# A SwiGLU trunk in float32: input products of pairs of chunks by seven block products in place of eight

## The chip, the core and the metric

The kernel runs on one core of one Trainium2 chip. The metric is the device time of one execution in microseconds, given as the median of the runs. "The span" is the time between the first and last recorded instruction of one profiled execution. Engines are named as in the profile: PE (TensorE), DVE (VectorE), ACT (ScalarE), POOL (GpSimd) and SP (SyncE); SP and POOL issue the transfers here.

## What is computed

One inference step of a trunk of two layers for 544 tokens (512 of a prompt, 32 of samples). Each layer is a SwiGLU block, a mixer (retention in the first layer, RG-LRU in the second) and another SwiGLU block, each followed by a layer norm. All is float32; the model width is 1024 and the hidden width of SwiGLU 2816.

```python
def swiglu(x, w_in, w_out):
    g, u = jnp.split(x @ w_in, 2, axis=-1)
    return (jax.nn.silu(g) * u) @ w_out

def trunk(...):
    for layer in range(DEPTH):
        x = layer_norm(ALPHA * x + 0.5 * swiglu(x, ffn1_w_in[layer], ffn1_w_out[layer]), ...)
        m = retention_mixer(x, ...) if layer % N_MIXERS == 0 else rglru_mixer(x, ...)
        x = layer_norm(ALPHA * x + m, ...)
        x = layer_norm(ALPHA * x + 0.5 * swiglu(x, ffn2_w_in[layer], ffn2_w_out[layer]), ...)
```

## The kernel before

**Layout.** Activations are feature-major: the 1024 features are 8 chunks `k` of 128 partitions, and the 544 tokens lie on the free axis in two halves of 272 (`HF`). `X` holds the input of a block as a high and a low part, `Z` the residual, and `H` in the area `ARR` the hidden chunks, high and low. A product of float32 operands is three float32r products of those parts, `mm3`: high by high, high by low, low by high, all adding in one of 8 banks of PSUM.

**Weights.** They come as units of 128x1024 float32 (512 KB, 8 tiles of 128x128). `pump` lets SP load a unit into one of 4 `raw` tiles (L445); `split` lets ACT write its high part and `low` lets DVE write its low part (`raw` minus high) into one of 6 `hl` tiles, or into one of two more in `ARR` (`ext`). Units are loaded and split in the order in which `use` first names them.

**A SwiGLU block** (`ffn`). The 22 hidden chunks of 128 come in three parts (`PARTS`). In a part, each chunk and half takes one gate and one up product of 8 steps (24 matmuls of 128x272 each); ACT makes the silu of the gate (`ev_g`), DVE multiplies (`ev_u`), ACT writes the high part of the hidden chunk, DVE the low part. Then the part's output products follow, 8 chunks `m` by two halves, n steps (3n matmuls) each for a part of n chunks. `zev` adds their results into `Z`; with the first part it makes the residual, by two DVE operations on `X`'s parts. In the first part the first four chunks run all in half 0 first and then in half 1, since half 1's layer norm (`ln`) is still on its way. In the last part the last four `m` run half 0 first, then half 1, so that half 0's layer norm runs beside half 1's products.

**Order.** The order on each engine is fixed when the program is written. `Flow` walks through the list of products (`job`, `together`, `gangs`: some products go step by step together) with a model of the engines' clocks, and everything else is a generator that is resumed when its inputs are modelled to be there. Each engine then runs its own list in order and waits by semaphores.

Of the kernel before, what the change touches and what calls it, by code (L numbers as in the profile page):

```python
# [25 lines left out]
P = 128  # L26
# [9 lines left out]
PARTS = [(0, 8), (8, 15), (15, 22)]  # L36
FH = 8
RH, DK, DV = 4, 256, 512
# [7 lines left out]
N_RAW = 4  # L46
N_HL = 6
EXT0 = 8832
# [8 lines left out]
N_EXT = 2  # L57
# [4 lines left out]
def band():  # L62
    """input chunks that feed each output chunk of the block-diagonal gates"""
# [13 lines left out]
# the recurrent block after its first projections: projections (x), gates (g), output gate (p)  # L77
# [18 lines left out]
# parameter columns  # L96
# [7 lines left out]
# constant columns  # L104
# [95 lines left out]
def build(tc, D, O):  # L200
# [9 lines left out]
    X = sbt("X", 2, KC, TOK, dt=F32R)  # L210
# [6 lines left out]
    WARM = sbt("WARM", 512, dt=mybir.dt.bfloat16)  # L217
    NCV = sbt("NCV", RC, 27)
    NLR = sbt("NLR", RC, 9)
    # work areas of the phases: float32r operands and float32 data  # L220
    AR_R, AR_F = 13696, 7860
    ARR = sbt("ARR", AR_R, dt=F32R)
    ARF = sbt("ARF", AR_F)
    banks = deque((pp.tile([P, 512], F32, name=f"bank{i}"), 0.0) for i in range(8))

# [562 lines left out]
    def ffn(l, w, g, final=False, extra=None):  # L788
# [41 lines left out]
        if extra:  # L830
            do(extra)
# [923 lines left out]
```

## Time and profile before

| | |
|---|---|
| median of 3 runs | 2389.86 us (2389.68 to 2391.5) |
| span of the profiled execution | 2387.8 us |
| PE busy | 2368.8 us (99%), 18394 matmuls |
| DVE busy | 1299.4 us (54%) |
| ACT busy | 876.6 us (37%) |
| POOL busy | 19.8 us (1%) |
| transfers of SP (q1) | 232.06 MB, 31.5% of 16 engines' span |
| granted TensorE clock | nine tenths or more of full speed in all 40 slices |

Busy time is the time in which an engine has at least one instruction under way. Matmuls overlap, so the mean duration of one is longer than the distance from one to the next; the distance is read from a window: its length by the number of matmuls in it.

### The profile page before, as it was taken

Reading aid. Unit: us, or ns where it says so; the run is one execution under the profiler, and the core shown is the slowest. Engines: PE = TensorE matmul, PEld = TensorE weight load, DVE = VectorE, ACT = ScalarE, POOL = GpSimd, SP = SyncE. Lnnn points to the kernel's source line nnn. Section 1 sums busy time; section 2 is a strip of 40 time slices with the busy share of each in tenths; the row PEclk is TensorE's granted clock in tenths of the full one; section 3 lists DMA queues with packets and bytes.
Section 4 is the critical chain, followed back from the end, with each engine's and each line's share of the span. In section 5 each row is a group of like instructions: output and inputs, shape, how many; then the busy total and the mean of one; then the engine's idle time right before and its main releaser. Section 6 shows DMA issues by size and latency. Waiting matters only on the chain.

```text
span 2387.8 us, 42745 instructions
## 1 busy us (share of the span) xinstructions
PE 2368.8 (99%) x18394; PEld 2329.8 (98%) x18394; DVE 1299.4 (54%) x2390; ACT 876.6 (37%) x1477; POOL 19.8 (1%) x51
## 2 busy tenths in 40 slices
PE   9999999999999999999999999999999999999997
PEld 9999999989899999999999999999999999999997
DVE  5343337767676777643333854333587776343336
ACT  4223223343434335422223442222358845223233
POOL 0000000000000000000000000000011000000000
PEclk9999999999999999999999999999999999999999
DMA  6222322244342543322232232322213223223221
GB/s 215 88 88 87 92 89 63 68 153 136 126 162 85 177 150 122 123 86 88 88 89 89 63 106 89 89 89 85 84 53 92 90 89 124 89 89 89 80 63 39
DMA packets 68751, 236.86 MB, mean 99 GB/s; under 512 B 7456, under 2 KB 11552, under 8 KB 68560
## 3 DMA queue, kind: packets, MB, share of 16 engines
q1 hardware_dynamic: 68016, 232.06, 31.5%
q8 instruction: 144, 2.36, 0.4%
q0 software_dynamic: 544, 2.05, 0.3%
q14 instruction: 47, 0.39, 0.0%
HBM read 212.79 MB, written 21.29 MB: 98 GB/s over the span
## 4 chain that ended last, share of the span: by engine, by line
PE 97%; DVE 2%; ACT 0%; DMA 0%; issue 0%; SPq 0%; ACTq 0%; DVEq 0%
PE bank L353 95%; PE bank L357 1%; DVE ARF L324 0%; DVE Z L315 0%; PE bank L361 0%; DVE SM L333 0%; DVE raw L319 0%; DVE Z L319 0%; DMA Z<-in_x 0%; DVE SM L315 0%; ACT ARF L296 0%; ACT SM L296 0%; DVE ARF L315 0%; DVE X L319 0%; DVE SM L337 0%
## 5 line engine op out<-in xcount | busy, mean ns | idle before, releaser
L353 PE MATMUL bank<-X,hl 128*128 128x272 f32 x8640 | 1110.4, 288 | 3.6 <-DVE ARF L324 2.4
L353 PEld LDWEIGHTS bank<-X,hl 128*128 128x128 f32 x8640 | 1094.9, 188 | 8.8 <-DVE ARF L324 3.0
L315 DVE TENSOR_TENSOR hl<-raw,hl 128x1024 fp32r<-128x1024 f32 (+1 forms) x326 | 395.7, 1220 | 424.2 <-ACT hl L296 424.0
L353 PE MATMUL bank<-ARR,hl 128*128 128x272 f32 x4632 | 601.9, 289 | 0.0
L353 PEld LDWEIGHTS bank<-ARR,hl 128*128 128x128 f32 x4632 | 589.6, 188 | 3.5 <-issue 0.8
L296 ACT ACTIVATE hl<-raw 128x1024 fp32r<-128x1024 f32 (+1 forms) x326 | 341.5, 1054 | 504.5 <-PE bank L353 445.1
L296 ACT ACTIVATE ARR<-ARF 128x272 fp32r<-128x272 f32 (+9 forms) x290 | 128.4, 450 | 487.7 <-DVE ARF L319 414.4
L353 PE MATMUL bank<-X,ARR 128*128 128x272 f32 x2304 | 300.8, 288 | 0.0
L353 PEld LDWEIGHTS bank<-X,ARR 128*128 128x128 f32 x2304 | 293.6, 188 | 0.5 <-DVE ARR L315 0.2
L353 PE MATMUL bank<-ARR 128*128 128x272 f32 (+4 forms) x1556 | 244.7, 309 | 0.0
L353 PEld LDWEIGHTS bank<-ARR 128*128 128x128 f32 (+1 forms) x1556 | 216.8, 188 | 13.5
L315 DVE TENSOR_TENSOR ARR<-ARF,ARR 128x272 fp32r<-128x272 f32 (+9 forms) x290 | 133.2, 468 | 122.8 <-ACT ARR L296 122.2
L319 DVE SCALAR_TENSOR_TENSOR ARF<-bank,ARF 128x272 f32<-128x272 f32 x176 | 77.0, 437 | 196.1 <-PE bank L353 191.5
L315 DVE TENSOR_TENSOR Z<-Z,bank 128x272 f32<-128x272 f32 (+1 forms) x238 | 115.3, 491 | 100.0 <-PE bank L353 90.5
L296 ACT ACTIVATE ARF<-bank 128x272 f32<-128x272 f32 (+4 forms) x314 | 122.5, 398 | 92.2 <-PE bank L353 43.9
L315 DVE TENSOR_TENSOR ARR<-raw,ARR 128x1024 fp32r<-128x1024 f32 (+1 forms) x74 | 88.4, 1196 | 122.4 <-ACT ARR L296 122.3
L296 ACT ACTIVATE ARR<-raw 128x1024 fp32r<-128x1024 f32 (+1 forms) x74 | 76.5, 1036 | 134.5 <-PE bank L353 129.0
L353 PEld LDWEIGHTS bank<-hl,X 128*128 128x128 f32 x768 | 93.9, 188 | 4.5 <-issue 1.7
L353 PE MATMUL bank<-hl,X 128*128 128x256 f32 x768 | 95.5, 282 | 1.2 <-DVE X L319 0.8
L296 ACT ACTIVATE ARF<-Z 128x272 f32<-128x272 f32 (+1 forms) x86 | 39.2, 458 | 108.6 <-DVE Z L315 106.7
L315 DVE TENSOR_TENSOR ARF<-ARF 128x272 f32<-128x272 f32 (+1 forms) x146 | 61.3, 446 | 4.7 <-ACT ARF L296 2.5
L315 DVE TENSOR_TENSOR Z<-Z,ARF 128x272 f32<-128x272 f32 (+1 forms) x116 | 50.7, 473 | 10.9 <-ACT ARF L296 10.4
(83 smaller groups left out, 844.2 us busy)
## 6 DMA issues: line engine op xcount, KB each, us to landing
raw<-in_win SPq DMA_DIRECT2D x173, 512.0 KB, 3.5
raw<-in_wout SPq DMA_DIRECT2D x88, 512.0 KB, 3.6
raw<-in_sret SPq DMA_DIRECT2D x32, 512.0 KB, 3.7
out_rets<-raw SPq DMA_DIRECT2D x32, 512.0 KB, 3.5
raw<-in_rwin_v SPq DMA_DIRECT2D x16, 512.0 KB, 3.6
raw<-in_rwin_kq SPq DMA_DIRECT2D x16, 512.0 KB, 3.6
raw<-in_rwin_g SPq DMA_DIRECT2D x16, 512.0 KB, 3.6
raw<-in_rwout SPq DMA_DIRECT2D x16, 512.0 KB, 4.3
```

What stands on the lines that cost most here:

```text
L296: nc.scalar.activation(out=out, in_=in_, func=func, scale=scale, **kw)
L315: nc.vector.tensor_tensor(out=out, in0=a, in1=b, op=op)
L319: nc.vector.scalar_tensor_tensor(out=out, in0=a, scalar=s, in1=b, op0=op0, op1=op1)
L353: nc.tensor.matmul(out, lhsT=a, rhs=b, start=start, stop=stop)
L357: nc.tensor.matmul(out, lhsT=a, rhs=b, start=start, stop=stop)
```

## The change

Chunks 0 to 3 of a block stay as they were. The other 18 are taken as 9 pairs. For a pair, gate and up are each a product of 2x2 blocks: the weights are split in 2 chunks by two halves of the 8 features chunks (`a11`, `a12`, `a21`, `a22`), the input in two halves of the features by the two halves of the tokens. Strassen's scheme in Winograd's form makes it of seven block products, each 4 steps (12 matmuls of 128x272) for gate and for up: `s1`, `a11`, `s2`, `a12`, `s3`, `s4`, `a22`. They use three pairs of banks, (s1, s4), (a11, a12) and (s2, s3, a22), and the later ones of a bank keep adding onto what it holds after its earlier state has been read. DVE puts the results together in `GT` and `UT` (`ev`), and `finish` makes the hidden chunks of the pair from columns of both chunks and both halves at once.

The sums of weight blocks (s1 = a21 + a22, s2 = s1 + a11, s3 = a11 + a21, s4 = s2 + a12) are made in the `raw` tiles: once the tile's own content has been split, GpSimd issues a DMA that adds the next block from DRAM onto it (`add_block`). A pair takes 4 loads, 4 such DMAs and 7 splits. The sums of the input blocks are made by `sums` once for a block; the operand of a22 takes the place of `X`'s half 1, chunks 0 to 3.

Along with this, `PARTS` becomes 8, 8 and 6 chunks; there are 6 `raw` tiles; the additional `hl` tiles serve the four plain chunks and the recurrent block alone; the load of s1 is issued two places earlier; the layer norm leaves the full float32 input in `Z` (`xf`, an ACT operation for each chunk and half), from which `zev` makes the residual by one DVE operation; and the first two output products of every part go step by step together. `X` and `ARR` are one tile, `BIG`.

```diff
-PARTS = [(0, 8), (8, 15), (15, 22)]
+PARTS = [(0, 8), (8, 16), (16, 22)]
+NE = 4
-N_RAW = 4
+N_RAW = 6
+EXT = (10880, 12928, 8704, 13056)
+AHEAD = 2
...
+    def order_loads():
+        loads.extend(u for u in units if not u["prev"])
+        for i, u in enumerate(list(loads)):
+            if u["more"] is not None:
+                loads.remove(u)
+                loads.insert(max(1, i - AHEAD), u)
...
-            if not u["state"]:
+            if u["next"]:
+                v = u["next"]
+                v["raw"] = raw
+                add_block(v, v["ap"], t)
+            elif not u["state"]:
...
+    def add_block(u, ap, t):
+        nc.gpsimd.dma_start(out=u["raw"], in_=ap, accum_op=ALU.add)
+        st["dma"] = max(st["dma"], t + 1.5, fl.pe + 1.5) + 2.0
+        u["t_raw"] = st["dma"] + 1.2
+        note("dma", (), u["raw"], u["t_raw"])
...
+        if not final and g != 4:
+            for c in range(KC):
+                yield pace()
+                z = Z[:, c, sl]
+                t = act(z, z, dep=fl.ev["x", g, c, half], func=AF.Identity, bias=pcol("ln_b", 8 * li + c))
+                fl.set(("xf", g, c, half), t)
...
-            if first and not (last and m):
+            if first and not last:
+                yield ("xf", g - 1, m, half)
+                t = stt(z, z, ALPHA, b[:, :HF], ALU.mult, ALU.add, dep=t)
+                release(b, t)
...
+        def sums():
+            yield ("lnd", g, 1) if g else 0.0
+            for c in range(KC):
+                for half in range(2):
+                    yield ("xf", g, c, half)
+            o = LNB[g].o
+            T = ar(o, 3, HK * HF).rearrange("p i (c n) -> p i c n", c=HK)
+            b11, b12, b21, b22 = (Z[:, k:k + HK, h * HF:h * HF + HF] for k in (0, HK) for h in (0, 1))
+            def parts(name, src, hi, lo, t):
+                t = act(hi, src, dep=t)
+                t = tt(lo, src, f(hi), ALU.subtract, dep=t)
+                fl.set(("tf", g, name), t)
+            t = tt(T[:, 0], b11, b12, ALU.subtract)
+            t1 = tt(T[:, 1], b12, b22, ALU.subtract)
+            parts("s1", T[:, 0], TF[:, 0, 0], TF[:, 0, 1], t)
+            yield pace()
+            t = tt(T[:, 2], b11, T[:, 1], ALU.subtract)
+            parts("s2", T[:, 2], TF[:, 1, 0], TF[:, 1, 1], t)
+            yield pace()
+            parts("s3", T[:, 1], TF[:, 2, 0], TF[:, 2, 1], t1)
+            yield pace()
+            t = tt(T[:, 0], b21, T[:, 2], ALU.subtract)
+            yield ("plain", nin)
+            parts("a22", T[:, 0], X[:, 0, 0:HK, HF:TOK], X[:, 1, 0:HK, HF:TOK], t)
...
+            def ev(form, i, b, t):
+                b = b[:, :HF]
+                yield t
+                if form == "a11":
+                    t = act(R[i], b, dep=t)
+                    fl.set(("rd", nin, j, "a12", i), t)
+                elif form == "s1":
+                    yield ("rd", nin, j, "a12", i)
+                    if j > NE:
+                        yield ("hf", nin, j - 2)
+                    t = tt(B1[i], b, R[i], ALU.add, dep=t)
+                    fl.set(("rd", nin, j, "s4", i), t)
+                elif form == "s2":
+                    yield ("rd", nin, j, "a12", i)
+                    if j > NE:
+                        yield ("hf", nin, j - 2)
+                    t = tt(B0[i], b, R[i], ALU.subtract, dep=t)
+                    fl.set(("rd", nin, j, "s3", i), t)
+                elif form == "s3":
+                    yield ("rd", nin, j, "s4", i)
+                    t = tt(B1[i], b, B1[i], ALU.subtract, dep=t)
+                    fl.set(("rd", nin, j, "a22", i), t)
+                elif form == "a22":
+                    t = tt(A1[i], b, R[i], ALU.subtract, dep=t)
+                    fl.set(("c21", nin, j, i), t)
+                elif form == "s4":
+                    yield ("rd", nin, j, "s3", i)
+                    t = tt(B0[i], b, B0[i], ALU.subtract, dep=t)
+                    fl.set(("c12", nin, j, i), t)
+                else:
+                    if j > NE:
+                        yield ("hf", nin, j - 2)
+                    if i:
+                        yield ("c11", nin, j)
+                        t = stt(A0[1], b, 0.5, A0[0], ALU.mult, ALU.mult, dep=t)
+                        fl.set(("h11", nin, j), t)
+                    else:
+                        t = act(A0[0], b, dep=t, func=AF.Silu)
+                        fl.set(("c11", nin, j), t)
+                return t
...
+            def finish():
+                for i in range(2):
+                    for k in ("c12", "c21"):
+                        yield (k, nin, j, i)
+                    yield ("rd", nin, j, "a22", i)
+                    if i == 0:
+                        ts = act(GT[:, HF:], GT[:, HF:], dep=fl.ev["c21", nin, j, 0], func=AF.Silu)
+                yield ("h11", nin, j)
+                t = stt(UT[:, HF:], UT[:, HF:], 0.5, GT[:, HF:], ALU.mult, ALU.mult, dep=ts)
+                hh, hl = H[:, 0, c:c + 2], H[:, 1, c:c + 2]
+                u2 = UT.rearrange("p (c n) -> p c n", c=2)
+                t = act(hh, u2, dep=t)
+                t = tt(hl, u2, f(hh), ALU.subtract, dep=t)
+                for m in (j, j + 1):
+                    for half in range(2):
+                        fl.set(("h", nin, m, half), t)
+                fl.set(("hf", nin, j), t)
...
+            def run():
+                fl.spawn(finish())
+                banks_of = {}
+                for form, bk in (("s1", 0), ("a11", 1), ("s2", 2), ("a12", 1), ("s3", 2), ("s4", 0), ("a22", 2)):
+                    u, mv = units_of[form], moving(form)
+                    for i in range(2):
+                        start = (bk, i) not in banks_of
+                        if start:
+                            banks_of[bk, i] = acq_main()
+                        else:
+                            fl.need(("rd", nin, j, form, i))
+                        b = banks_of[bk, i]
+                        for k in range(HK):
+                            need_unit(u)
+                            xh, xl, e = mv(k)
+                            fl.need(e)
+                            off = (HK * i + k) * P
+                            wt = u["hl"]
+                            mm3(b[:, :HF], wt[:, 0, off:off + P], wt[:, 1, off:off + P], xh, xl, start and k == 0, k == HK - 1, not start)
+                            used(u)
+                            fl.poll()
+                        fl.spawn(done(form, i, b, fl.pe + 0.1))
...
+                reg("s1", ap=win[blk["a21"]], more=win[blk["a22"]])
+                if last:
+                    last()
+                reg("a11", ap=win[blk["a11"]])
+                reg("s2", ap=win[blk["a11"]], prev=us["s1"])
+                reg("a12", ap=win[blk["a12"]])
+                reg("s3", ap=win[blk["a21"]], prev=us["a11"])
+                reg("s4", ap=win[blk["a12"]], prev=us["s2"])
+                last = lambda reg=reg, blk=blk: reg("a22", ap=win[blk["a22"]])
...
+            if hf == 0:
+                for half in range(2):
+                    gangs([x for j in js[:NE] for x in gu(j, half)], FGA if g else 1)
+                do(lambda: (fl.set(("plain", nin), fl.pe), st.update(ext=())))
+                js = js[NE:]
+            for j, us in pair_units(js[::2]):
+                pair(j, us, hf)
...
+                jobs.append(lambda m=m, half=half, hf=hf, n=n, rhs=rhs:
+                            job(wtiles(nout + str(hf), wout[hf], m * n, range(n)), rhs, half,
+                                zev(m, half, hf == 0, hf == 2, (li, g + 1, final), count, guard)))
+            gangs(jobs, 2)
```

PE, first block, chunks 4 and 5 (a row is a product: the bank it fills, its operands, the shape, and the number of matmuls). Before:

```order
L353 MATMUL bank0_81<-X_61,hl0_67 128x272 x24
L353 MATMUL bank1_82<-X_61,ARR_79 128x272 x24
L353 MATMUL bank2_83<-X_61,hl0_67 128x272 x24
L353 MATMUL bank3_84<-X_61,ARR_79 128x272 x24
L353 MATMUL bank4_85<-X_61,ARR_79 128x272 x24
L353 MATMUL bank5_86<-X_61,hl1_68 128x272 x24
L353 MATMUL bank6_87<-X_61,ARR_79 128x272 x24
L353 MATMUL bank7_88<-X_61,hl1_68 128x272 x24
```

and after, from s1 to the first of s4:

```order
L359 MATMUL bank0_81<-BIG_61,hl0_69 128x272 x12
L359 MATMUL bank1_82<-BIG_61,hl0_69 128x272 x12
L359 MATMUL bank2_83<-BIG_61,hl1_70 128x272 x12
L359 MATMUL bank3_84<-BIG_61,hl1_70 128x272 x12
L359 MATMUL bank4_85<-BIG_61,hl2_71 128x272 x12
L359 MATMUL bank5_86<-BIG_61,hl2_71 128x272 x12
L359 MATMUL bank2_83<-BIG_61,hl3_72 128x272 x12
L359 MATMUL bank3_84<-BIG_61,hl3_72 128x272 x12
L359 MATMUL bank4_85<-BIG_61,hl4_73 128x272 x12
L359 MATMUL bank5_86<-BIG_61,hl4_73 128x272 x12
L359 MATMUL bank0_81<-BIG_61,hl5_74 128x272 x12
```

Eight products of 24 matmuls became fourteen of 12 (the second of s4 and two of a22 follow), and a unit of weights now serves 24 matmuls instead of 48.

DVE, end of the first block's last input products. Before, from the last chunk's evictions (its ARR is the low part of `H`) to the first output product:

```order
L319 SCALAR_TENSOR_TENSOR ARF_80<-bank5_86,ARF_80 128x272
L315 TENSOR_TENSOR ARR_79<-ARF_80,ARR_79 128x272
L315 TENSOR_TENSOR ARR_79<-raw1_64,ARR_79 128x1024
L319 SCALAR_TENSOR_TENSOR ARF_80<-bank7_88,ARF_80 128x272
L315 TENSOR_TENSOR ARR_79<-ARF_80,ARR_79 128x272
L315 TENSOR_TENSOR Z_62<-Z_62,bank0_81 128x272
```

and after, from the last pair's evictions (GT and UT lie in ARF, `H` in BIG):

```order
L320 TENSOR_TENSOR ARF_80<-bank6_87,ARF_80 128x272
L320 TENSOR_TENSOR hl5_74<-raw3_66,hl5_74 128x1024
L320 TENSOR_TENSOR ARF_80<-bank7_88,ARF_80 128x272
L324 SCALAR_TENSOR_TENSOR ARF_80<-ARF_80 128x816
L320 TENSOR_TENSOR BIG_61<-ARF_80,BIG_61 128x1088
L320 TENSOR_TENSOR Z_62<-Z_62,bank0_81 128x272
```

The last pair's hidden chunks are now finished in one operation of 816 and one of 1088 columns behind the last eviction, where each half of a chunk was finished by itself.

## Rows read from the trace of the kernel before

**Rows 1.** The page: span, busy time (share, instructions), chain that ended last by engine

```profile
span 2387.8 us, 42745 instructions
...
PE 2368.8 (99%) x18394; PEld 2329.8 (98%) x18394; DVE 1299.4 (54%) x2390; ACT 876.6 (37%) x1477; POOL 19.8 (1%) x51
...
PE 97%; DVE 2%; ACT 0%; DMA 0%; issue 0%; SPq 0%; ACTq 0%; DVEq 0%
```

**Rows 2.** Waits of PE: engine and line waited for: us, times, longest

```profile
PE bank L353 <- DVE ARF L324: 2.4, 3, 0.9
...
PE bank L353 <- ACT X L296: 1.1, 2, 0.7
```

**Rows 3.** Windows: length, busy PE, PEld, DVE, ACT, POOL (instructions), clock, DMA, GB/s

```profile
200.00:300.00 100.00, 100.00 (x799) 100.00 (x798) 34.61 (x53) 24.37 (x35) 0.00 (x0) 1.00 0.30 90
2000.00:2300.00 300.00, 300.00 (x2392) 300.00 (x2391) 115.12 (x176) 84.03 (x127) 0.00 (x0) 1.00 0.31 94
2355.00:2374.00 19.00, 18.79 (x147) 18.41 (x145) 15.13 (x37) 8.90 (x19) 0.00 (x0) 1.00 0.13 46
```

**Rows 4.** Groups by line and shape: busy us, mean ns of one | idle before

```profile
L353 PE MATMUL bank<-X,hl 128*128 128x272 f32 x8640 | 1110.4, 288 | 3.6 <-DVE ARF L324 2.4 <-ACT X L296 0.7 <-DVE X L315 0.4
...
L315 DVE TENSOR_TENSOR hl<-raw,hl 128x1024 fp32r<-128x1024 f32 x324 | 394.3, 1223 | 420.8 <-ACT hl L296 420.6
L296 ACT ACTIVATE hl<-raw 128x1024 fp32r<-128x1024 f32 x324 | 340.3, 1057 | 502.9 <-PE bank L353 445.1 <-issue 39.8 <-DMA raw<-in_sret 8.5
...
L296 ACT ACTIVATE ARF<-bank 128x272 f32<-128x272 f32 x262 | 100.9, 389 | 84.0 <-PE bank L357 39.5 <-PE bank L353 39.4 <-DVE ARR L315 2.0
...
L315 DVE TENSOR_TENSOR ARF<-bank,ARF 128x272 f32<-128x272 f32 x76 | 29.4, 434 | 14.6 <-PE bank L357 7.4 <-PE bank L353 7.0
...
L296 ACT ACTIVATE Z<-Z,PR 128x272 f32<-128x272 f32 x15 | 8.6, 608 | 8.5 <-DVE Z L315 8.5
...
L315 DVE TENSOR_TENSOR Z<-Z 128x1088 f32<-128x1088 f32 x5 | 6.5, 1292 | 0.2
...
L296 ACT ACTIVATE Z<-Z 128x1088 f32<-128x1088 f32 x5 | 5.6, 1113 | 0.1
```

**Rows 5.** Timeline of PE behind the first block and ahead of the recurrent one

```profile
422.00 4.14 PE L353 MATMUL bank<-X,hl 128*128 128x272 f32 x30
426.53 0.50 PE L353 MATMUL bank<-hl,X 128*128 128x256 f32 x2 [0.39 <-ACT X L296]
427.84 4.42 PE L353 MATMUL bank<-hl,X 128*128 128x256 f32 x35 [0.82 <-DVE X L319]
...
1771.15 1.12 PEld L353 LDWEIGHTS bank<-X,hl 128*128 128x128 f32 x8 [0.30 <-DVE X L319]
```

**Rows 6.** Timeline of the third SwiGLU block's start (start us, us, engine, line, ...)

```profile
1349.46 2.79 PE L353 MATMUL bank<-X,hl 128*128 128x272 f32 x21
...
1373.15 1.32 DVE L319 SCALAR_TENSOR_TENSOR X<-Z,PR,X 128x272 fp32r<-128x272 f32 x3
```

**Rows 7.** DMA: queue shares (whole, then 200 to 300 us), issues, POOL's loads

```profile
q1 hardware_dynamic: 68016, 232.06, 31.5%
...
q1 hardware_dynamic: 2448, 8.91, 29.7%
...
raw<-in_win SPq DMA_DIRECT2D x14, 512.0 KB, 3.5
raw<-in_wout SPq DMA_DIRECT2D x3, 512.0 KB, 3.6
...
ARF<-in_dt POOLq DMA_DIRECT2D x4, 320.0 KB, 3.3
...
ARF<-in_cs POOLq DMA_DIRECT2D x1, 544.0 KB, 4.0
...
L1047 POOL DMA_DIRECT2D ARF<-in_dt x4: 536/537/543, 423.8 to 817.4; - x4
...
DMA to landing us min/median/max: 3.2/3.3/5.6
```

More of the change, by code (lines that the diff above doesn't have):

```diff
@@ L350, in pe, with mm @@
         h.append((0, 512, "pe", fl.pe, True))
-    def mm(out, a, b, start, stop):
-        nc.tensor.matmul(out, lhsT=a, rhs=b, start=start, stop=stop)
+    def mm(out, a, b, start, stop, cont=False):
+        nc.tensor.matmul(out, lhsT=a, rhs=b, start=start, stop=stop, skip_group_check=cont)
         pe(out, a, b, size(b), a.shape[0])
@@ L419, in split @@
         raw = u["raw"]
-        parts = [slice(i * UW // u["cut"], (i + 1) * UW // u["cut"]) for i in range(u["cut"])]
+        cut = u.setdefault("cut", 1)
+        parts = [slice(i * UW // cut, (i + 1) * UW // cut) for i in range(cut)]
         t = max(u["t_raw"], t_hl + 0.1)
@@ L698, in ev @@
                 yield ("zd", g, m, half)
-            if first and not (last and m):
+            if first and not last:
+                yield ("xf", g - 1, m, half)
+                t = stt(z, z, ALPHA, b[:, :HF], ALU.mult, ALU.add, dep=t)
+                release(b, t)
+            elif first and not m:
                 t = stt(z, f(X[:, 0, m, sl]), ALPHA, b[:, :HF], ALU.mult, ALU.add, dep=t)
@@ new lines, in pair_units, with reg @@
+        def pair_units(js):
+            res = []
+            last = None
+            for j in js:
+                n0 = 2 * NE + 2 * (j - NE)
+                blk = {"a11": n0, "a12": n0 + 1, "a21": n0 + 2, "a22": n0 + 3}
+                us = {}
+                def reg(form, key=j, us=us, **kw):
+                    us[form] = use((nin, "pair", key, form), n=2 * HK, **kw)
+                reg("s1", ap=win[blk["a21"]], more=win[blk["a22"]])
[7 more added lines that the diff above has]
+                last = lambda reg=reg, blk=blk: reg("a22", ap=win[blk["a22"]])
+                res.append((j, us))
+            last()
+            return res
@@ L830, in ffn @@
         if extra:
             do(extra)
+        do(lambda: st.update(ext=(2, 3)))
+        do(lambda: fl.spawn(sums()))
         for hf, (j0, j1) in enumerate(PARTS):
             js = list(range(j0, j1))
-            ne = 4 if hf == 0 else 0
-            order = [(j, 0) for j in js[:ne]] + [(j, 1) for j in js[:ne]] + [(j, h) for j in js[ne:] for h in (0, 1)]
             def gu(j, half):
-                return [lambda: job(wtiles(nin, win, (2 * j) * KC, range(KC), True), xrhs(g), half, ev_g(j, half)),
-                        lambda: job(wtiles(nin, win, (2 * j + 1) * KC, range(KC), True), xrhs(g), half, ev_u(hf, j, half))]
@@ L839, in ffn @@
-            for part, n in ((order[:ne], FGA if g else 1), (order[ne:], FGB if ne and g else 1)):
-                gangs([x for jh in part for x in gu(*jh)], n)
+                return [lambda: job(wtiles(nin, win, (2 * j) * KC, range(KC), (2, 3)), xrhs(g), half, ev_g(j, half)),
+                        lambda: job(wtiles(nin, win, (2 * j + 1) * KC, range(KC), (2, 3)), xrhs(g), half, ev_u(hf, j, half))]
+            if hf == 0:
[3 more added lines that the diff above has]
+                js = js[NE:]
@@ L1584, in rhs @@
                 return XH[:, 0, k, hs(half)], XH[:, 1, k, hs(half)], ("yr", k, half)
-            job(wtiles("co", D["cwout"], m * RC, range(RC), True), rhs, half, zev(m, half, True, True, (4, g + 1, False), count))
+            job(wtiles("co", D["cwout"], m * RC, range(RC), (0, 1)), rhs, half, zev(m, half, True, True, (4, g + 1, False), count))
+        do(lambda: st.update(ext=()))
     ffn(0, 0, 0)
```

117 lines of the change are left out of this document (70 added, 47 removed).

## Prediction, made before the result was known

> **What bounds the kernel now.** I read the busy shares first, then the chain of waits, then TensorE's waits. TensorE is busy for 2368.8 of the 2387.8 us, VectorE for 54%, ScalarE for 37% [rows 1], and 97% of the chain that ended last is TensorE's own [rows 1]. The time that TensorE spends waiting for another engine inside the program comes to a few us; its two largest entries that the change touches are 2.4 us and 1.1 us [rows 2]. So a removed matmul is worth one matmul pitch, as long as nothing that the change adds becomes later than TensorE. In a plain stretch of input and output products 2392 matmuls take 300.00 us and in another 799 take 100.00 [rows 3]: 125.4 and 125.2 ns each, at a granted clock of 1.00 (the level of 2.4 GHz). The mean duration of 288 ns in the grouped row [rows 4] is not the price, since matmuls overlap. In such a stretch VectorE works 38%, ScalarE 28% and the DMA engines 31% of the time [rows 3], so there is room, though not without end.
>
> The span is 2387.8 us, and the median of the runs 2389.9: about 2.1 us lie outside the span. I make the sum against the span and add 2.1.
>
> **1. Matmuls removed.** A pair of chunks took 2 chunks x 2 products x 2 halves x 24 = 192 matmuls of 128x272 and takes 7 x 24 = 168. There are 9 pairs in each of four SwiGLU blocks: 36 x 24 = 864 fewer. 864 x 125.4 ns = **-108.3 us**. Everything removed was on the path, so this is also the most that the change can give: 2389.9 - 108.3 = 2281.6.
> The row puts the pitch of 272 columns at 125.4 ns. The Trainium skill, "TensorE: Matmul & The Clock Gate", section "Back-to-back issue gap", gives N/2.4 + 2.5 ns for a single warm matmul, 115.8 ns here; by it this term would be an estimated -100.1 us. The trace disagrees by 8% and decides.
>
> **2. The end of each part.** Output products need the hidden chunks. Before, the last chunk's gate and up were evicted product by product; now a pair's four chunks of results become final only after the last product (a22), and then come in a row a VectorE eviction (434 ns), a product of 816 columns (between the 434 ns of 272 and the 1292 ns of 1088: 1.0 us), ScalarE's high part of 1088 (1.11 us) and VectorE's low part of 1088 (1.29 us) [rows 4]: 3.8 us, and about 4.2 with the weight split of 1.22 us that the order puts between the evictions. Cover: the two first output products go step by step together, so (n-2) chunks x 2 x 3 matmuls stand ahead of the first one that needs the pair. For parts of 8 chunks that is 36 x 0.1254 = 4.5 us, which hides it; for the part of 6, 24 x 0.1254 = 3.0, short by 1.2. Four blocks: **+4.8** (0 if the split isn't in the way and ScalarE answers at once, 30 if every one of the 12 part ends loses 2.5).
>
> **3. A shorter last part (7 chunks to 6).** The layer norm of half 0 is covered by the last four products of half 1. They shrink by 4 x 3 = 12 matmuls, 1.5 us. TensorE already waits there: 0.39 and 0.82 us behind the first block, 0.30 us ahead of the recurrent block [rows 5]; so what is taken from the cover is waited for. There are three such places, of which I charge two in full: **+3.0** (0 to 4.5). At the kernel's end the seven last products shrink by 21 matmuls, 2.6 us, while VectorE is busy for 15.13 of 19.00 us there [rows 3]; half of it: **+1.3** (0 to 2.6).
>
> **4. The residual.** Z gets the layer norm's bias on ScalarE (64 more operations of 608 ns [rows 4], 38.9 us) and 80 VectorE operations leave. The first 32 of them stand between the layer norms of the two halves. There is little slack: half 1's last chunks of X are written until 1374.5, and half 0's four plain chunks, started at 1349.46 [rows 6], last 192 x 0.1254 = 24.1 us, until 1373.5. I take 0.75 us at each of four norms: **+3.0** (0 to 10).
>
> **5. Sums of activations.** The operands of s1, s2, s3 and a22 are sums of quarters of the input, made after half 1's norm and needed after 4 plain chunks in both halves (48.2 us: from 1349.5 to 1397.7). From 1374.5 that leaves 23 us; the eight bias operations of half 1 (4.9 us) and four rounds of 1.29 + 1.11 + 1.29 us make about 20 when nothing else runs between. Tight, **+1.0** (0 to 6).
>
> **6. Splits and evictions of a pair.** 108 more weight splits (7 instead of 4 for each pair). One pair lasts 168 x 0.1254 = 21.07 us. VectorE in it: 7 x 1.223 + 11 evictions x 0.434 + 1.0 + 1.29 = 15.6 us; ScalarE: 7 x 1.057 + 2 copies x 0.389 + about 1.2 for two silus + 1.11 = 10.5. Neither is full. A bank is written again after three groups of 12 matmuls, 4.5 us behind the end of the group that must be evicted first; an eviction takes 0.43 and may stand behind two splits (2.4). Taken at **0**; if it isn't covered, one split of 1.22 us for each pair shows up (rival C).
>
> **7. The accumulating DMAs.** 144 of them, 4 for each pair, issued by GpSimd; no row of before shows one. From below: a plain load of 512 KB by SyncE lands after 3.5 us, GpSimd's plain loads of 320 and 544 KB after 3.3 (3.2 to 5.6) and 4.0, with 0.54 us of issue [rows 7]. The share of a plain load in the 16 engines is 0.297 x 100 us / 17 loads = 1.75 us [rows 7]. From above I have nothing but the work itself: the destination must be read as well as written, and the pieces may go slower. The weights of a pair pass through the chain: s1 split (1.06 + 1.22), accumulate (L), s2 split, accumulate (L), s4's high part, then the next pair's s1. This is 2 x (2.3 + L) + 1.1, and stays below 21.07 while L, from readiness to landing, is up to **7.7 us**. In engine time: 4 x 1.75 + 4a, below 21.07 while a is up to **3.5 us**, twice a plain load. I take L = 4 to 6 and a = 1.75 to 3.5, nearest to GpSimd's own rows: hidden, **0**. If a pair takes more, the products made ahead help: six split buffers hold up to 5 of a pair's 7 splits at a part's start, 10 to 15 us. A gain isn't to be had here: TensorE is not waiting for weights now.
>
> **Sum.** -108.3 + 4.8 + 3.0 + 1.3 + 3.0 + 1.0 = -95.2: span 2292.6, time **2295**.
>
> **Rivals.**
> (A) The accumulate costs exactly twice a plain load. Then the DMA engines have 7.0 + 14.0 = 21.0 us of work in a pair's 21.07, against 31% now, and a load or an accumulate stands behind another one: one plain load (1.75 us) uncovered in every third pair is 36 x 0.58 = 21 us: **2316**. For it: the destination is a second operand. Against: the lead at part starts. By the Trainium skill, "Collectives: The Full Stack", section "The bandwidth ceiling: the fold count and why AG ≠ RS ≠ AR", an add in a DMA needs two source reads for each chunk and runs at half the rate of a copy; no row here shows it.
> (B) Slower: the accumulate costs three times a plain load (5.25 us) or lands after some 11 us. A pair takes 28.0 us, 6.9 more than its matmuls. Part by part (2, 4 and 3 pairs) with 10 us of lead each: 3.8 + 17.6 + 10.7 = 32.1, in four blocks 128 us: 2295 + 128 = **2423**. It decides where 9 pairs lose 23.8 + 30 us in a block: 6.0 for each pair, a pair of 27.0, that is a = 5.0 us or L = 10.7. TensorE would wait for splits whose ScalarE half waits for a DMA. For it: no row of the operation. Against: plain loads land in 3.5 to 4.0.
> (C) A jam in the queues: in the fixed order VectorE and ScalarE stand at a split whose sum hasn't landed, and the evictions behind it come late; one split of 1.2 us for each pair: 36 x 1.2 = 43, **2338**.
> (D) The change does not do what it says: shorter groups (12 matmuls for 24) cost TensorE at each change of bank. 36 x 14 = 504 groups would have to lose 0.19 us each to eat the gain: **2390**. Against: in the stretch of 2392 matmuls the changes of bank are in the pitch, and runs of 30 show no idle time between them [rows 3, 5].
>
> **How the numbers follow.** Forecast 0.66, A 0.13, C 0.08, B 0.11, D 0.02. The range goes from the full gain without a stall (2281) to C (2338): B, D and a little beyond either end are left out, together under 0.2. About 0.2% (5 us) is what a measurement of this kernel can tell from no change. Faster: forecast, A and C, with a part of D: 0.88; the same 0.01; slower: B, 0.11.
>
> **What would show it.** 864 fewer matmuls of 128x272 at 125 ns (1). A wait of TensorE, about 1.2 us, for VectorE's low part at the first output product of each third part, and none at the others (2). Longer waits for X behind the norms (3, 4) and at the first s1 or a22 of a block (5). Pairs in 21.1 us, with VectorE 74% busy (6). Accumulates that land within 7.7 us, with ScalarE's splits not waiting for them on the path, and a queue of GpSimd whose engine time is 144 x 1.75 to 3.5 us (7). Wrong would be: a pair much longer than 21.1 us (B, C), or a pitch in pairs above 125 ns (D).

## The result and the profile after

The changed kernel takes 2353.1 us (2351.3 to 2355.2 in four runs) against 2390.5 us: a ratio of 0.984, with a 95% interval of 0.983 to 0.986. It is 37 us faster, where 95 were forecast; 2353.1 lies above the stated range of 2281 to 2338. The page of the profiled execution:

```profile
span 2351.3 us, 41831 instructions
...
PE 2289.0 (97%) x17530; PEld 2238.5 (95%) x17530; DVE 1532.3 (65%) x2630; ACT 1021.0 (43%) x1557; POOL 143.5 (6%) x195
...
q1 hardware_dynamic: 68016, 232.06, 30.0%
q0 software_dynamic: 21280, 77.56, 19.4%
...
PE 89%; DVE 7%; ACT 3%; issue 1%; DMA 0%; SPq 0%; ACTq 0%; DVEq 0%
...
raw<-in_win POOLq DMA_DIRECT2D x144, 512.0 KB, 5.7
```

The 864 matmuls are gone (18394 to 17530), and against [rows 1] TensorE's share of the chain fell from 97% to 89%: 10% of it is VectorE and ScalarE now, and none is DMA. TensorE's waits say who:

```profile
PE bank L359 <- ACT BIG L301: 20.8, 17, 6.7
PE bank L359 <- DVE BIG L320: 12.3, 14, 0.9
PE bank L359 <- ACT ARF L301: 5.7, 4, 3.2
```

BIG holds the operands of matmuls. In [rows 2] the largest such wait was 2.4 us in three pieces; now the first two are 33 us in 31 pieces, in front of operands that ScalarE (high parts) and VectorE (low parts) finish late. The next view is of windows (length, busy time of PE, PEld, DVE, ACT and POOL with instructions, granted clock, DMA share, GB/s), first a stretch of nothing but pairs, then five in which TensorE waits:

```profile
160.00:230.00 70.00, 70.00 (x559) 70.00 (x558) 47.44 (x66) 33.16 (x40) 8.70 (x10) 1.00 0.74 184
100.00:110.00 10.00, 8.71 (x68) 8.28 (x67) 5.37 (x7) 4.00 (x4) 0.87 (x1) 1.00 0.77 192
350.00:360.00 10.00, 7.19 (x39) 6.60 (x39) 4.90 (x8) 2.08 (x5) 0.56 (x1) 0.83 0.38 129
410.00:420.00 10.00, 7.29 (x36) 6.89 (x35) 9.99 (x25) 4.48 (x9) 0.00 (x0) 0.66 0.13 34
1370.00:1380.00 10.00, 5.53 (x45) 5.31 (x43) 5.10 (x8) 6.16 (x11) 1.41 (x2) 0.94 0.69 112
1380.00:1390.00 10.00, 7.08 (x33) 6.77 (x34) 8.75 (x10) 5.77 (x7) 0.00 (x0) 0.55 0.37 118
```

Within the pairs nothing waits: 559 matmuls in 70.00 us are 125.2 ns each, as in [rows 3], with VectorE at 68%, ScalarE at 47% and the DMA engines at 74%. All the loss lies in a few places between them, and the granted clock, which was 1.00 before up to the last matmuls, falls behind the longer waits.

To find those places, take the time from the start of each matmul to the start of the next, less the pitch of its shape in undisturbed stretches, and add it up. Over the run this sum is 71 us larger after than before; 864 pitches are 108.3, and the tail behind the last matmul grew by 1.4: 108.3 - 71 - 1.4 = 36, the difference of the two spans (2387.8 - 2351.3 = 36.5). The 71 us by place, what the low clock takes from the matmuls included:

| place | lost more than before | of it clock | forecast |
|---|---|---|---|
| ends of the 12 parts (8 x 1.8, 4 x 3.3 to 4.9) | 32.3 | 3.2 | 4.8 |
| start of the third block, 1375 to 1403 | 15.5 | 3.8 | 1.0 for all four blocks |
| starts of the second and fourth blocks | 4.3 | | in the 1.0 |
| layer norms (410, 895 to 931, 1325, 1723 to 1748) | 14.6 | 2.6 | 3.0 + 3.0 |
| start and end of the kernel, and what is too small to place | 4.5 | 1.5 | 1.3 |

### The profile page after: what moved, and what is told of

It is laid out like the page before. It is cut to its first block, busy times and chain, and to the rows that moved or that the text cites. A ratio compares the mean times of both kernels' runs of the same rounds, so it can differ in the third digit from the quotient of the medians.

```text
span 2351.3 us, 41831 instructions
## 1 busy us (share of the span) xinstructions
PE 2289.0 (97%) x17530; PEld 2238.5 (95%) x17530; DVE 1532.3 (65%) x2630; ACT 1021.0 (43%) x1557; POOL 143.5 (6%) x195
## 3 DMA queue, kind: packets, MB, share of 16 engines
q0 software_dynamic: 21280, 77.56, 19.4%
## 4 chain that ended last, share of the span: by engine, by line
PE 89%; DVE 7%; ACT 3%; issue 1%; DMA 0%; SPq 0%; ACTq 0%; DVEq 0%
PE bank L359 87%; DVE hl L320 1%; PE bank L363 1%; ACT hl L301 1%; ACT BIG L301 1%; DVE ARF L320 1%; DVE BIG L320 1%; DVE ARF L324 1%; DVE Z L324 1%; DVE Z L320 1%; ACT ARF L301 0%; DVE ARF L329 0%; DVE BIG L324 0%; DVE SM L338 0%; PE bank L367 0%
## 5 line engine op out<-in xcount | busy, mean ns | idle before, releaser
L359 PE MATMUL bank<-BIG,hl 128*128 128x272 f32 x15096 | 1949.7, 290 | 44.0 <-ACT BIG L301 18.9
L359 PEld LDWEIGHTS bank<-BIG,hl 128*128 128x128 f32 x15096 | 1920.5, 189 | 63.9 <-ACT BIG L301 22.7
L320 DVE TENSOR_TENSOR hl<-raw,hl 128x1024 fp32r<-128x1024 f32 (+1 forms) x490 | 596.1, 1221 | 493.6 <-ACT hl L301 491.0
L301 ACT ACTIVATE hl<-raw 128x1024 fp32r<-128x1024 f32 (+1 forms) x490 | 514.1, 1055 | 751.3 <-PE bank L359 572.1
L320 DVE TENSOR_TENSOR BIG<-ARF,BIG 128x272 fp32r<-128x272 f32 (+11 forms) x198 | 136.6, 702 | 103.2 <-ACT BIG L301 102.6
L320 DVE TENSOR_TENSOR ARF<-bank,ARF 128x272 f32<-128x272 f32 (+3 forms) x460 | 186.0, 436 | 14.6 <-PE bank L363 7.9
L359 PE MATMUL bank<-BIG 128*128 128x272 f32 (+5 forms) x1172 | 194.1, 316 | 0.2 <-DVE ARF L329 0.2
L359 PEld LDWEIGHTS bank<-BIG 128*128 128x128 f32 (+3 forms) x1172 | 167.9, 188 | 13.8 <-DVE ARF L329 0.7
L359 PE MATMUL bank<-hl,BIG 128*128 128x256 f32 (+2 forms) x1024 | 146.6, 300 | 2.7 <-ACT BIG L301 1.9
L359 PEld LDWEIGHTS bank<-hl,BIG 128*128 128x128 f32 (+1 forms) x1024 | 127.3, 179 | 13.9 <-ACT BIG L301 2.1
L301 ACT ACTIVATE ARF<-Z 128x272 f32<-128x272 f32 (+1 forms) x86 | 39.4, 458 | 103.8 <-DVE Z L320 101.1
```

The source lines that it names most:

```text
L301: nc.scalar.activation(out=out, in_=in_, func=func, scale=scale, **kw)
L320: nc.vector.tensor_tensor(out=out, in0=a, in1=b, op=op)
L359: nc.tensor.matmul(out, lhsT=a, rhs=b, start=start, stop=stop, skip_group_check=cont)
```

## The experiments

The theory was that these are separate short chains of VectorE and ScalarE that TensorE waits for, each to be mended by itself. The rival was that the stream of weights (DMA, splits) is late as a whole, and that a wait that is taken away comes back at the next place. Times are medians; the changed kernel has 2353.1. (The expectations, written before this table, count half of each stretch at the low clock as lost. TensorE was idle in part of them, so that 18.5 us at the third block there are 15.5 here.)

### The end of a part

The timeline of VectorE, then ScalarE, then TensorE, at the end of the first part (start us, length us, engine, line, operation, count, idle time before and what ended it):

```profile
99.33 0.78 DVE L320 TENSOR_TENSOR ARF<-bank,ARF 128x272 f32<-128x272 f32 x2
101.15 1.23 DVE L320 TENSOR_TENSOR hl<-raw,hl 128x1024 fp32r<-128x1024 f32 x1 [1.03 <-ACT hl L301]
102.29 0.43 DVE L320 TENSOR_TENSOR ARF<-bank,ARF 128x272 f32<-128x272 f32 x1
102.83 1.01 DVE L324 SCALAR_TENSOR_TENSOR ARF<-ARF 128x816 f32<-128x816 f32 x1
105.01 1.29 DVE L320 TENSOR_TENSOR BIG<-ARF,BIG 128x1088 fp32r<-128x1088 f32 x1 [1.18 <-ACT BIG L301]
```

```profile
100.05 1.06 ACT L301 ACTIVATE hl<-raw 128x1024 fp32r<-128x1024 f32 x1 [1.90 <-PE bank L359]
101.02 0.87 ACT L301 ACTIVATE ARF<-ARF 128x816 f32<-128x816 f32 x1
103.87 1.11 ACT L301 ACTIVATE BIG<-ARF 128x1088 fp32r<-128x1088 f32 x1 [1.98 <-DVE ARF L324]
```

```profile
93.72 10.96 PE L359 MATMUL bank<-BIG,hl 128*128 128x272 f32 x86
105.03 0.39 PE L359 MATMUL bank<-BIG,hl 128*128 128x272 f32 x1 [0.36 <-ACT BIG L301]
106.36 0.89 PE L359 MATMUL bank<-BIG,hl 128*128 128x272 f32 x5 [0.94 <-DVE BIG L320]
```

The pair's last product is done at about 100.2. VectorE stands at a weight split whose high part ScalarE makes only then (100.05 to 101.1), and the eviction that everything waits for comes behind it, at 102.29. The chain is over at 106.3: 6.1 us, not 4.2. Two ways to mend it, one on either side.

**More cover (e1).**

```diff
-            gangs(jobs, 2)
+            gangs(jobs, 4)
```

> The first four output products of each part go step by step together, in place of the first two. Theory: the lost time at the ends of parts is a chain of 6.2 us behind the last product of a pair (eviction, product, high part, low part, with a weight split in between), of which the cover hides 4.5 us (8 chunks) or 3.0 us (6 chunks). Four products make the cover 9.0 and 6.0 us: the eight waits of 1.72 us go, the four of 3.24 us shrink to 0.2, and the clock doesn't fall behind them (3 x 1.7 us): 13.8 + 12.2 + 5.1 = 31 us less than the changed kernel, 2322. Rival: TensorE there follows a stream of weights or evictions that is late as a whole; then the wait moves behind the gang and the time stays within 5 us of 2353.

Measured: 2332.2 us, 21 less. The eight waits of 1.72 us are gone, and of the four of 3.24 no more than 0.3 is left, as the theory said. But in the last part TensorE now waits longer for the layer norm of half 0, here for the first of three:

```profile
380.83 0.62 PE L363 MATMUL bank<-ARF,CT 128*128 128x272 f32 x2
385.60 0.51 PE L359 MATMUL bank<-hl,BIG 128*128 128x256 f32 x2 [4.16 <-ACT BIG L301]
```

At the first norm this only takes the place of the 7 us that the changed kernel loses there (at 410); at the second and third norm 6.1 and 3.1 us more are lost than in the changed kernel, the low clock included, and another 4.6 in the mixer behind the first block (476 to 492). The start of the third block, which wasn't edited, loses 5.9 less. Together these make most of the 10 us by which the gain falls short. The rival, that the wait moves behind the gang, doesn't hold for the part ends; it holds for the last part, in another form.

**A shorter chain (e2).** `hold` is set at the start of a part's last a22 and cleared behind the pair's low part; `pump` begins no split while it is set.

```diff
+            if st["hold"]:
+                break
```

> No weight split is begun between the start of a part's last a22 product and the end of the pair's low part. Theory: the split between the two evictions of a22 costs the chain about 2 us, since VectorE stands at it until ScalarE has made its high part; without it the chain is 4.2 us, the eight ends of 8 chunks lose 0 in place of 1.72, the four of 6 chunks 1.3 in place of 3.24, and the clock falls less: 20 to 26 us less than the changed kernel, 2327 to 2333, unless the delayed split of output weights is itself missed. Rival: the four steps of the chain alone are longer than they were taken, then no more than 5 us.

Measured: 2329.3 us, 24 less, inside the range. VectorE and ScalarE at the same place now:

```profile
97.92 1.29 DVE L320 TENSOR_TENSOR ARF<-bank,ARF 128x272 f32<-128x272 f32 x3
98.80 0.89 ACT L301 ACTIVATE ARF<-ARF 128x816 f32<-128x816 f32 x1 [2.05 <-DVE ARF L320]
99.72 1.01 DVE L324 SCALAR_TENSOR_TENSOR ARF<-ARF 128x816 f32<-128x816 f32 x1 [0.51 <-ACT ARF L301]
100.76 1.11 ACT L301 ACTIVATE BIG<-ARF 128x1088 fp32r<-128x1088 f32 x1 [1.08 <-DVE ARF L324]
...
101.91 1.29 DVE L320 TENSOR_TENSOR BIG<-ARF,BIG 128x1088 fp32r<-128x1088 f32 x1 [1.18 <-ACT BIG L301]
```

The chain runs through without a split. At the eight ends of 8 chunks the loss is 0.0 to 0.2 us, at the four of 6 chunks 1.5, where 1.3 was worked out: some 25 us less at the ends in all. New losses of 1.4 to 1.8 us at 481, 1006 and 1152 take a part of it back. The mis-sized term was the split.

**Three together in the last part alone (e9, on top of e8 below).**

```diff
-            gangs(jobs[:8], 2)
+            gangs(jobs[:8], 3 if hf == 2 else 2)
```

> The three edits of e8 and, in the last part alone, three output products step by step together in place of two. Theory: without a split in it the chain of a pair is 4.2 to 4.5 us, and three products of the part of 6 chunks cover 4.5 us: the four waits of 1.5 us that e8 still has there go, 6 us less than e8, 2318, with the norms' waits as they are. Rival: more products together shift work out of the cover of the second norm, as four did (4.3 us at three norms in place of 2), then the same or up to 6 us more than e8.

Measured: 2331.3, 7 us more than e8, a little beyond the rival's 6. The rival was right in kind: the 6-chunk ends lose next to nothing any more, and TensorE waits 4.2 us for the norm at 381 and 3.4 at the two others, with 6.8 us at the low clock behind each. The norm that is late is half 0's, as in e1. The traces show where its time goes. VectorE in e9, at the eviction of half 0's last output product (Z) and the steps behind it, then the same eviction in the changed kernel:

```profile
373.04 1.22 DVE L320 TENSOR_TENSOR hl<-raw,hl 128x1024 fp32r<-128x1024 f32 x1 [2.18 <-ACT hl L301]
374.18 0.43 DVE L320 TENSOR_TENSOR Z<-Z,bank 128x272 f32<-128x272 f32 x1
...
376.12 2.36 DVE L320 TENSOR_TENSOR hl<-raw,hl 128x1024 fp32r<-128x1024 f32 x2 [0.68 <-ACT hl L301]
```

```profile
381.33 0.44 DVE L320 TENSOR_TENSOR Z<-Z,bank 128x272 f32<-128x272 f32 x1 [1.00 <-PE bank L359]
```

In the changed kernel the eviction follows its product at once, and one weight split stands among the norm's steps; in e9 the eviction stands behind a split that waits for ScalarE, and more splits stand behind it. That is what the ends of parts showed, at another place. No run kept the splits away from there, so what they cost at the norms is read from the traces and not shown by an experiment.

### The start of the third block

The lines of VectorE, ScalarE and TensorE in the changed kernel, in order of time:

```profile
1377.08 0.51 ACT L301 ACTIVATE Z<-Z,PR 128x272 f32<-128x272 f32 x1
...
1379.71 2.48 DVE L320 TENSOR_TENSOR ARF<-Z 128x1088 f32<-128x1088 f32 x2
1381.03 1.11 ACT L301 ACTIVATE BIG<-ARF 128x1088 fp32r<-128x1088 f32 x1 [2.49 <-DVE ARF L320]
...
1382.19 0.60 PE L359 MATMUL bank<-BIG,hl 128*128 128x272 f32 x1 [6.66 <-ACT BIG L301]
...
1394.65 1.28 DVE L320 TENSOR_TENSOR ARF<-Z,ARF 128x1088 f32<-128x1088 f32 x1
1395.97 1.11 ACT L301 ACTIVATE BIG<-ARF 128x1088 fp32r<-128x1088 f32 x1 [6.58 <-DVE ARF L320]
...
1398.36 5.81 PE L359 MATMUL bank<-BIG,hl 128*128 128x272 f32 x32 [3.24 <-ACT ARF L301]
```

The last bias operation on Z ends at 1377.6; fourteen of the sixteen run after half 1's norm, from 1353.1 on, in between evictions and splits. The first sum follows at 1379.7, and TensorE, which needs its high part, has waited 6.7 us. Between 1389.4 and 1394.6 VectorE works through some 28 small operations (10 columns, 0.17 us each), the rates of the recurrent block, which the kernel before also computes here; behind them comes the fourth sum, ScalarE stands 6.6 us at that sum's high part, and the eviction of a11 is behind ScalarE's stand.

**The rates elsewhere (e4).** `lru_rates` among the first part's output products:

```diff
+            if extra and hf == 0:
+                do(extra)
```

> The small computation of the recurrent block's rates (28 VectorE operations on 10 columns, two table loads) leaves the start of the third block and stands among the output products of its first part. Theory: at 1388 to 1394.5 it stands in front of the fourth sum on VectorE, whose high part holds up ScalarE's copy of a11 behind it; without it the wait of 3.4 us and one stretch at the low clock (1.7 us) go: 5 us less than the changed kernel. The first wait of 6.8 us stays. Rival: the fourth sum waits for the end of the plain products anyway, then 0.

Measured: 2350.6, 2.5 less, which is no more than the spread of the runs; the trace tells more. The second wait went (the block's start lost 10.5 us in place of 15.5), the first stayed at 6.8; but the moved operations cost 3.5 us where they went, in front of the next part's first pairs (0.98, 1.29 and 0.95 us between 1528 and 1553).

**The bias operations at once, at all norms (e3).**

```diff
-                yield pace()
```

> The sixteen operations that put the bias onto Z are issued right behind each half's layer norm, without spacing. Theory: the sums of input blocks in the third block come 7 us late because the bias operations before them are spread over 24 us behind evictions and splits; issued at once the sums are early enough, and the waits of 6.8 and 3.4 us at 1375 and 1395 with the low clock behind them (18.5 us in all) go, those of 1 to 2 us in the second and fourth block too; the norms may lose up to 4 us as ScalarE is occupied between the halves: 12 to 20 us less than the changed kernel. Rival: the work of the sums itself is what is too long, then within 4 us of it.

Measured: 2367.0, 14 us more: the forecast had the wrong sign. The wait at 1375 did go, so the late bias operations were its cause. But new waits came: 6.8 us at 1397, where the rates now stand on VectorE in front of the first pair's evictions, 2.2 and 3.1 at the start of the fourth block, 2.1 at the second's. The first of them:

```profile
1404.34 1.96 PE L359 MATMUL bank<-BIG,hl 128*128 128x272 f32 x7 [6.61 <-DVE ARF L320]
```

With the low clock behind them they are more than what was won.

**The bias operations at once, at the third block alone (e10), with e2's `hold`; and the same with the rates moved (e8).**

```diff
+                if g != 3:
+                    yield pace()
```

> As e8, but the rates are computed where the change leaves them, at the start of the third block. Theory: the two waits in the third block have two causes, the late bias operations (about 9 us with the low clock) and the rates on VectorE and their table loads on ScalarE (5 us or more): 2329 - 9 = 2320 to 2326, near e8, since the moved rates cost e8 3.6 us among the output products. Rival: both waits have one cause, then the same as e2 (2329) or more.

> Three edits together: no split behind a part's last a22 (2329 by itself), the rates computed among the first output products of the third block, and the bias operations of the norm ahead of the third block at once. Theory: the three waits are separate ones. The third block's start, which lost 18.5 us, keeps 3 to 5; the moved rates cost 3 where they go: 2329 - 14 + 3 = 2318, or 2315 to 2322. Rival: with the bias operations at once the splits and evictions of the first pair come late instead (as with all four norms at once), then 2327 or more.

Measured: e10 2324.9 and e8 2323.9, a ratio of 0.9725 (0.971 to 0.974) to the kernel before: 66 us less than before and 29 less than the changed kernel, the least of those run. e10 is inside its range, e8 missed its own (2315 to 2322). Both are 4 to 5 us below e2 (2329.3) with runs that overlap, so what they add to `hold` rests on the traces more than on the times. Of the changed kernel's 15.5 us at this place, e10 keeps 11.7, most of it in one wait with the low clock behind it. Its VectorE and its TensorE:

```profile
1377.80 0.17 DVE L329 TENSOR_SCALAR SM<-SM 128x10 f32<-128x10 f32 x1 [0.33 <-ACT SM L301]
...
1382.87 0.25 DVE L329 TENSOR_SCALAR SM<-SM 128x10 f32<-128x10 f32 x2
1383.03 1.13 DVE L320 TENSOR_TENSOR ARF<-bank,ARF 128x272 f32<-128x272 f32 x3
```

```profile
1383.87 2.41 PE L359 MATMUL bank<-BIG,hl 128*128 128x272 f32 x9 [7.78 <-DVE ARF L320]
```

The evictions of the first pair stand behind the rates, and TensorE behind the evictions. e8 has two waits of 2.1 and 2.8 us in its place, 9.3 us lost with the clock; it pays 3.6 us where the rates are now and 3.2 in a new wait at the second block's start. So the two causes are separate, as e4 and e3 said, but what they give doesn't add up. That the planner orders the queues anew with each edit is the likely reason; it was not shown.

### The layer norms

**The last part of 6 without the rest (e5).** The kernel before, with

```diff
-PARTS = [(0, 8), (8, 15), (15, 22)]
+PARTS = [(0, 8), (8, 16), (16, 22)]
```

> The kernel before with parts of 8, 8 and 6 chunks in place of 8, 7 and 7, nothing else. Theory: a last part of 6 takes 1.5 us from the cover of the layer norm of half 0 at three places, where TensorE waits already, and 2.6 us from the cover of the last norm: 3 to 6 us more than before (2393 to 2396), and a stretch at the low clock behind a longer wait would add 1.7 to 3.4. Rival: the norms' cover has slack that the waits of before don't show, then within 1 us of before.

Measured: 2395.1, a ratio of 1.002 (1.001 to 1.003) to before, 5.2 us more. TensorE at the norm behind the first block in this kernel:

```profile
428.04 0.50 PE L353 MATMUL bank<-hl,X 128*128 128x256 f32 x2 [1.90 <-ACT X L296]
429.35 2.87 PE L353 MATMUL bank<-hl,X 128*128 128x256 f32 x13 [0.81 <-DVE X L319]
```

against 0.39 and 0.82 in [rows 5], and a stretch of 3.4 us at the low clock behind it. The changed kernel has the same two waits at the same place, to the digit:

```profile
412.10 0.50 PE L359 MATMUL bank<-hl,BIG 128*128 128x256 f32 x2 [1.90 <-ACT BIG L301]
413.41 10.84 PE L359 MATMUL bank<-hl,BIG 128*128 128x256 f32 x66 [0.81 <-DVE BIG L324]
```

The shorter part is the whole cause of the waits there. What the clock adds differs: 3.4 us at the lower level behind them in e5, 6.8 in the changed kernel.

**The bias operations between the norms (e11).** As e2, with half 0's bias operations behind half 1's norm:

```diff
+            if not half:
+                yield ("lnd", g, 1)
```

> As e2, but the eight bias operations of half 0 wait until half 1's layer norm is done, so that ScalarE has none of them between the two norms. Theory: they cost the second half's norm little (under 1 us at each of four norms), since ScalarE waits for VectorE there, while the sums become later still: e2 plus 0 to 6 us. Rival: they are what holds the second half's norm (2.06 and 2.17 us at 402 and 924), then 4 to 8 us less than e2.

Measured: 2336.8, 7 us more than e2, 1 beyond the range. The waits at the norms are the same (1.90 and 0.81 at 404 to 407, 2.17 at 925); the first of them in this run:

```profile
405.90 0.50 PE L359 MATMUL bank<-hl,BIG 128*128 128x256 f32 x2 [1.90 <-ACT BIG L301]
```

So the bias operations do not hold the norms. They hold the sums: the start of the second block now loses 7.6 us in place of e2's 3.7.

### The accumulating DMAs

**Plain loads in their place (e6); each twice (e7).** The sums of weights aren't made in e6, and are other sums in e7, so neither computes the trunk.

```diff
-        nc.gpsimd.dma_start(out=u["raw"], in_=ap, accum_op=ALU.add)
+        nc.gpsimd.dma_start(out=u["raw"], in_=ap)
```

> GpSimd's 144 accumulating transfers are plain loads of the same blocks into the same tiles, so the sums of weights aren't made; all else is the changed kernel. Theory: the accumulates are hidden in the pairs (5.7 us to landing, below 7.7; 3.1 us of the engines each), so their price is next to nothing: 0 to 5 us less than the changed kernel, the small part at the first pairs of a block where ScalarE waits for them. Rival: the traffic of the accumulates is what makes operands late at the ends of parts and at the blocks' starts, then 20 us or more less.

> Each accumulating transfer is issued twice in a row onto the same tile, so the sums of weights are other ones. Theory: a pair hides accumulates until they land after 7.7 us or fill the engines. Twice in a row they land after 11 us, a pair's chain of splits takes 2 x (2.3 + 11.4) + 1.1 = 28.5 us and the engines 4 x 1.6 + 8 x 3.1 = 31 us, against 21.07 of matmuls; with 10 us of lead in each part 150 to 250 us more than the changed kernel, with TensorE waiting for splits. Rival: the lead of loads and splits is larger than 10 us for each part, then under 60 us more.

Measured: e6 2352.1, 1.0 less than the changed kernel, which is within the spread of the runs; its TensorE waits are the same. Queue of GpSimd and landing in e6:

```profile
q0 software_dynamic: 21280, 77.56, 10.5%
...
raw<-in_win POOLq DMA_DIRECT2D x144, 512.0 KB, 3.9
```

With 77.56 MB being 148 units of 512 KB (144 of them these transfers), a plain load takes 0.105 x 2348.5 / 148 = 1.67 us of the engines and an accumulate 0.194 x 2351.3 / 148 = 3.08, that is 1.85 times; it lands 1.8 us later (5.7 against 3.9) and TensorE doesn't see it.

e7 took 2880.4 in its one run, 527 us more, twice what the theory gave. TensorE waits for what ScalarE and VectorE make, and ScalarE for transfers:

```profile
PE bank L359 <- ACT ARF L301: 263.7, 37, 13.0
PE bank L359 <- DVE ARF L320: 126.8, 25, 6.5
...
ACT hl L301 <- DMA raw<-in_win: 891.3, 105, 15.3
```

The mechanism is the one expected, and the formula of the chain holds: two accumulates in a row (6.4 us to landing each, 0.9 of issue) make L about 13.7 and a pair 33 us, 12 more than its matmuls, which is 430 us for 36 pairs. The rest is the low clock (0.91 mean granted), which takes some 110 us more from the matmuls than in the changed kernel. What was wrong was the lead of 10 us for each part: the first block's second part, with four pairs, ends 197 us behind the first part's end, against 135 in the changed kernel, 15.5 more for each pair with the clock, so there is next to none.

## Why the prediction was wrong

The direction and the largest term were right, the size was not. Of the 58 us between 2295 and 2353.1, term 2 made 27.5, term 5 made 18.8, the norms (terms 3 and 4) 8.6, and the start, the end and what is too small to place 3.2; 11 us of all this are the clock's. Each of the two large misses by itself would have left the time within the range, whose upper end was rival C's alone and not a sum of the terms' upper bounds.

**1, the matmuls**: right. 864 fewer, at 125.2 ns in the pairs. The formula of the Trainium skill ("TensorE: Matmul & The Clock Gate", "Back-to-back issue gap"), an estimated 115.8 ns, is for a single matmul; the pairs, a stream, don't show it either. Rival D is answered too: with 12 matmuls to a group the pitch is the same.

**2, the ends of parts**: the step that failed most, 32.3 for 4.8. The four operations of the chain were sized rightly (0.43, 1.01, 1.11, 1.29 us). "About 4.2 with the weight split that the order puts between the evictions" was wrong: the split was charged about 0.4 us, and it costs 2, because VectorE doesn't only execute it but stands at it until ScalarE has made its high part, which itself starts only when TensorE gives an `hl` tile free. The order of instructions showed the split between the two evictions; what it didn't show is whose finish it waits for. The row of that operation in [rows 4] did: before 324 of them VectorE stood idle for 420.8 us, 420.6 of it for ScalarE, 1.3 us each. With 6.1 us in place of 4.2, all twelve ends lose, where four were charged. The term passed the upper bound of 30 that the prediction gave it, with the 3.2 us of the clock in it.

**3, the shorter last part**: 3.0 + 1.3 forecast; by itself, in the kernel before, 5.2. Right in mechanism and near in size, though not for the reasons given alone: at the norm behind the first block e5 loses 3.0 us more than before, 1.5 by the waits, as worked out, and the other 1.5 by the clock. In the changed kernel the norms lose 14.6; what of it is beyond this term (some 4 us at 895 to 931, behind the retention, and more at 1723 to 1748 than e5 has there) was not taken apart.

**4, the residual**: the place was wrong. The bias operations cost the norms nothing (e11); they cost the block's start, since the sums wait for all sixteen of them, and fourteen, where term 5 counts eight, ran behind half 1's norm.

**5, the sums**: 19.8 for 1.0, beyond the bound of 6. Two things failed. The 23 us of cover were compared with the work of the chain (20 us when nothing else runs), and the words "when nothing else runs between" were the error: evictions, splits and the sixteen bias operations share the two queues, and at the third block the recurrent block's rates too, which stand in the code of before at the same place and were not looked for.

**6, splits and evictions inside a pair**: right, 0. Rival C was about the wrong place: such jams exist, but at the first pair of a block and the last pair of a part, where queues are full of other work, not in each pair.

**7, the accumulating DMAs**: right, 1 us or nothing. L is 5.7 and a 3.08. Rival A's premise (twice a plain load) nearly holds at 1.85 times, and yet it costs nothing, since the engines are at 0.74 of their time in a pair. The half rate that the Trainium skill ("Collectives: The Full Stack", "The bandwidth ceiling: the fold count and why AG ≠ RS ≠ AR") gives for an add in a collective is near the 1.85 times of this case. Rival B's decision point was too lenient: it counted on a lead that e7 doesn't show.

**The clock** was in no term, without a reason given. At the kernel's start and at waits of 2 to 7 us in one piece, or several close together, it was granted at the lower level (1.2 GHz) for 3.4 to 10.2 us, 34 us in all up to the last matmul; the matmuls in them took 11 us longer than at full speed. That added 1.1 us to each of three part ends that waited 3.2 us, 3.8 to the 11.7 at the third block, and 2.6 to the 2.7 at the norm at 410. The price is not a fixed one: behind the same two waits of 1.90 and 0.81 us at that norm the lower level lasted 6.8 us in the changed kernel and 3.4 in e2 and e5, and did not come at all in e8 and e11.

## What to carry to other kernels

When a change removes work from a saturated engine, the loss to look for is at the seams: the first operand of each new phase, and the last result of each old one. There, add up not the durations of a chain but the queues it passes: for every instruction between two links ask which engine it will stand waiting for. And give each wait of a few us a second price, for the clock that may fall behind it: here from nothing to about as much as the wait itself.

## What the runs showed of the hardware

- An accumulating DMA of 512 KB (DRAM onto SBUF, float32) lands 5.7 us after its issue (5.3 to 10.9) and takes 3.08 us of the sixteen engines (the mean of the queue), a plain one by the same engine 3.9 (3.6 to 8.0) and 1.67. GpSimd is occupied for 0.87 us to issue it, and 0.53 for the plain one.
- The granted clock was 1.00 for the whole of the kernel before up to its last matmuls. In the changed one it fell to the lower level for 3.4 us behind the 3.2 us lost at 351 (0.83 in the window 350 to 360), for 6.8 us behind the norm at 410, and for 10.2 us from within the 6.8 us at 1375. The eight waits of 1.7 us behind the parts of 8 chunks left it at 1.00, and so did the 3.2 us lost at 1684.
